# One transformer block on one core: sums of the down projection's weight blocks moved behind the attention, and a planner's priorities set anew

## The chip, the core and the metric

The kernel runs on one core of a Trainium2 chip. The core has five engines with an instruction queue each: TensorE (PE in the profile; PEld is its loading of weights), VectorE (DVE), ScalarE (ACT), GpSimd (POOL) and SyncE (SP). SP does nothing but issue DMAs; ACT and POOL issue some as well. An engine works through its queue in order, so an instruction that waits holds up all that stand behind it. The metric is the device time of one execution in microseconds (us); lower is better.

## The reference

One block of a transformer with 512 tokens and a width of 1024, all in 32-bit floats:

```python
h = x
u = rmsnorm(h, norm_mix_g) @ w_in
c_q, c_kv, k_rope, q_nsa, kv_cmp, kv_slc, kv_win, gate_logits = split(u)
o_mla = mla_mixer(c_q, c_kv, k_rope, ...)        # latent attention, 8 heads
o_nsa = nsa_mixer(q_nsa, kv_cmp, kv_slc, kv_win, gate_logits, ...)   # sparse attention: compressed, selected, window
mixed = concatenate([rmsnorm(o_mla), rmsnorm(o_nsa)])
h = h + mixed @ w_out
f = rmsnorm(h, norm_ffn_g)
h = h + (silu(f @ w_gate) * (f @ w_up)) @ w_down   # w_gate, w_up: 1024 x 2816, w_down: 2816 x 1024
return rmsnorm(h, final_norm_g)
```

## The kernel before

Nearly every product is split for accuracy: each operand is parted into a rounded high part and the rest (w_hi and w_lo, xTh and xTl), and one product becomes three matmuls, which one helper writes at L168, L169 and L170. A weight block is loaded (w_raw, by SP at L405), cast to its high part (w_hi, L392) and subtracted to its low part (w_lo, L394 on DVE or L395 on POOL).

The stages follow each other in the trace as follows. From 0 to about 20 us x is normalized (scaling at L334) and transposed (L349), with products of the norm's gains with ones (L426) and small choice products (L535) in between. To about 105 us come the projections: x times the blocks of w_in, 24 matmuls of 512 columns for a block of 128 columns of weights; qs is the scaled query (L371). Among them is the hidden layer of the compressed keys and values (L715 and L717). Then follow the sparse attention (scores L894 and L895, scaling s on POOL at L840, transposes L845, values L879), and from about 197 us the latent attention's heads (scores L1185). w_out is multiplied first with the sparse half (oTh and oTl), then with the latent half (omh and oml); L1305 adds the result to h, and the norm's mean of the latent half is the product L1272. From about 300 us to 622 the feed-forward part runs: gate and up by a scheme that makes seven block products of eight (its loads at L1532, ACT's casts at L1580, DVE's subtractions at L1396, into w_unit), then down by a like scheme.

For down the scheme needs sums and differences of blocks of w_down. They are made memory to memory by sum_weights: six groups u of four sums T1, T3, T2, T4, each of 512 KB, as a copy from w_down into a tensor T in DRAM, issued by ACT (L1356), and a DMA that adds a second block onto it, issued by POOL (L1357). Each copy waits for the addition ahead of it, and the first for the loading of the gates (ga_loaded), so the 24 pairs are one chain; in the profiled execution it goes from 56.6 to 497 us. The loads of w_down's blocks in the second half (L1705) wait for their sum.

The order of the instructions is made by a planner in the kernel's own code. Each step is a Job with one or more ways (engine, estimated duration, function that writes the instructions), the jobs that it waits for, a priority and the buffers that it takes and frees. Plan.run keeps a clock for each engine; for each it picks, among the jobs whose start is earliest, the one with the lowest priority number, and writes its instructions there and then. So priorities and estimated durations fix every engine's order when the kernel is built, and the chip follows it whatever the real durations are. The dictionary PRI holds about thirty of the priorities and, as pdve, ppool and pact, an amount added for a job that could run on another engine too. SP also loads the bias (bn from ldr, L595) and the gates' rows (ga from gdr, L603) back out of DRAM, in eight DMAs at a time.

Of the kernel before, what the change touches and what calls it, by code (L numbers as in the profile page):

```python
# [13 lines left out]
OP = mybir.AluOpType  # L14
# [40 lines left out]
class Plan:  # L55
# [11 lines left out]
    def add(self, ways, fn=None, after=(), pri=0.0, takes=(), frees=(), lag=None):  # L67

        if fn is not None:
            ways = [(ways[0], ways[1] * (1.07 if ways[0] == "pe" and ways[1] < 1374 else 1.0), fn)]  # L70
        j = Job(ways, [a for a in after if a is not None], pri, takes, frees, lag)
        self.jobs.append(j)
        return j
# [13 lines left out]
    def run(self):  # L87
        busy = {}
        clock, ready, waiting = {"dma": 3500.0, "dma2": 3000.0}, [], list(self.jobs)
        while waiting or ready:  # L90
# [4 lines left out]
            for j in ready:  # L95
                if any(len(self.slots[s]) < j.takes.count(s) for s in j.takes):
                    continue
                for way in j.ways:
                    e = way[0]
                    issue = 1150 if e in ("dma", "dma2") else 0  # L100
                    t = max([clock.get(e, 0.0)] + [a.seen(e) + issue for a in j.after] + [min(self.slots[s]) + issue for s in j.takes])
                    best.setdefault(e, []).append((t + (PRI.get("p" + str(e), 0) if len(j.ways) > 1 else 0), j.pri, j, way, t))
            assert best, "no job can go on"
            picks = []
            for e, c in best.items():
                t0 = min(x[0] for x in c)
                picks.append(min((x for x in c if x[0] <= t0 + PRI["slack"]), key=lambda x: x[1]))
            _, _, j, way, t = min(picks, key=lambda x: (x[0], x[1]))
# [11 lines left out]

PRI = dict(k0=-5.4, q0=-12.1, v=51.3, ck=-13.0, k1=8.0, cv=-9.5, q1=-9.4, q2=-38.5, q3=12.6, mla=38.1, out=180.9, slack=0, pdve=20.1,
           ppool=72.3, pact=310.9, wload=-10.3, wsplit=-28.4, mkeys=-2.4, lat=-20.5, cmp=-18.4, cuse=94.3, use=17.0, sout=77.2, seven=183.9,
           xoff=-26.6, xstep=-35.5, bias=-61.8, sums=912.1, bout=-82.5, loff=-25.8, woff=-217.5, wstep=301.5)


@with_exitstack
def block_kernel(ctx: ExitStack, tc: tile.TileContext, I, out):
    nc = tc.nc  # L130
    ve, se, pe, gp, sy = nc.vector, nc.scalar, nc.tensor, nc.gpsimd, nc.sync
# [140 lines left out]
    add = plan.add  # L272
    late = {}

    def t_act(n, sb=False):
        return (95 if sb else 55) + 0.833 * n
# [4 lines left out]
    def t_dve(n):  # L281
        return 70 + 1.042 * n
# [18 lines left out]
    def load(dst, src, pri, after=()):  # L301
        n = int(np.prod(dst.shape)) * 4
        return add(("dma", max(n / 360.0, 480)), lambda: sy.dma_start(dst, src), after, pri, lag=950)
# [86 lines left out]
    def split_pieces(h, l, raw, n, after, pri, takes=(), frees=()):  # L390

        j = add([("act", t_act(n, True), lambda: se.copy(h(), raw())), ("dve", t_copy(n), lambda: ve.tensor_copy(h(), raw()))],  # L392
                None, after, pri, takes=takes)
        return add([("dve", t_dve(n), lambda: ve.tensor_tensor(l(), raw(), f(h()), op=OP.subtract)),  # L394
                    ("pool", t_pool(n), lambda: gp.tensor_tensor(l(), raw(), f(h()), op=OP.subtract))], None, [j], pri, frees=frees)  # L395

    def weight(pl, srcs, shape, pri, raw, part, nraw, npart, after=(), pieces=2, parts=None):
# [9 lines left out]
        def piece(c):  # L407
            return slice(c * shape[0] // pieces, (c + 1) * shape[0] // pieces)

        def room():  # L410
            w["h"], w["l"] = parts() if parts else [pl().tile([P] + list(shape), F32R, name=nm, tag=nm, bufs=npart) for nm in ("w_hi", "w_lo")]

        j = w["load"] = add(("dma", n * P * 4 / 360.0), start, after, pri + PRI["wload"], takes=[raw], lag=950)
        j = w["room"] = add((None, 0), room, [j], pri + PRI["wsplit"], takes=[part])
        return w, [split_pieces(lambda c=c: w["h"][:, piece(c)], lambda c=c: w["l"][:, piece(c)], lambda c=c: w["raw"][:, piece(c)], n // pieces,
                                [j], pri + PRI["wsplit"] + 0.1 * c, frees=[raw] if c == pieces - 1 else ()) for c in range(pieces)]

# [13 lines left out]
    def load_wl(u):  # L431
        sy.dma_start(wl_raw[:, u, :, 0:416], win[:, 2 * u:2 * u + 2, 0:416])
        sy.dma_start(wl_raw[:, u, :, 416:440], win[:, 2 * u:2 * u + 2, C_GATE:C_END])

    wl_ready = []
    for u in range(4):
        j = add(("dma", 1300), lambda u=u: load_wl(u), pri=-97 + (u if u < 3 else 4), lag=950)
        wl_ready += [split_pieces(lambda u=u, k=k: wl_parts[u][0][:, k], lambda u=u, k=k: wl_parts[u][1][:, k], lambda u=u, k=k: wl_raw[:, u, k],
                                  440, [j], -95 + PRI["woff"] + PRI["wstep"] * u) for k in range(2)]
    x_loaded = [x0] + [[load(xt[t], xv[:, t, :], (-94, -92, -91)[t - 1])] * 2 for t in range(1, NT)]  # L440
# [165 lines left out]
    ga_loaded = add(("dma", 3800), load_ga, bias1 + [p2_open], 6, lag=950)  # L606
# [475 lines left out]
    for t in range(NT):  # L1082
# [3 lines left out]
        def go(d=d, ts=ts):  # L1086
            d["o"] = bank("mm")
            mm3(d["o"], kvTh[:, ts], kvTl[:, ts], flat(late["uvh"]), flat(late["uvl"]), True, True)

        j = add(("pe", 640), go, uv_ready + lat_done, mpri + t, takes=["mm"])  # L1090
        vm_ready += split_values(lambda t=t: late["vm"][:, t], lambda d=d: d["o"].rearrange("p (h d) -> p h d", h=H), S, [j], mpri + t)
    for q in range(2):
        qc = slice(384 * q, 384 * q + 384)
        for t in range(NT):
# [17 lines left out]
            j = add(("pe", 480), lambda go=go: go(0), [uq_ready[q][0]] + lat_done, pri, takes=["mm"])  # L1112
            j = add(("pe", 480), lambda go=go: go(1), [j, uq_ready[q][1]], pri)
            j = add(("act", t_act(256)), lambda qd=qd, ov=ov: se.copy(qd()[:, :, 0:64], ov()[:, :, 0:64]), [j], pri)
            j = add(("dve", 480), rope, [j], pri, frees=["mm"])
# [192 lines left out]
    for nh in range(2):  # L1308
        for t in range(NT):
# [7 lines left out]
            j = None  # L1317
            for k in range(4):
                j = add(("pe", 640), lambda k=k, go=go: go(k), [j, wo[2 * nh + k // 2][1][k % 2]] + sparse_jobs, opri + 4 * nh + t, takes=["mm"] if k == 0 else (),
                        frees=["part2"] if t == NT - 1 and k % 2 else ())  # L1320
# [4 lines left out]
    for nh in range(2):  # L1325
        for t in range(NT):
# [7 lines left out]
            j = None  # L1334
            for k in range(4):
                j = add(("pe", 640), lambda k=k, go=go: go(k), [j, wo[4 + 2 * nh + k // 2][1][k % 2]] + latent_jobs, 300 + 4 * nh + t,
                        takes=["mm"] if k == 0 else (), frees=["part2"] if t == NT - 1 and k % 2 else ())
# [3 lines left out]

    wsum, wsum_done = {}, {}

    def sum_weights():
        wd = I["w_down"].rearrange("(q j p) (n c) -> p q j n c", j=2, p=P, n=2)
        last = [ga_loaded]
        for u in range(6):
            qs = slice(2 * u, min(2 * u + 2, 11))
            n = qs.stop - qs.start
            for name in ("T1", "T3", "T2", "T4"):  # L1350
                wsum[name, u] = dram.tile([P * n, 512], F32, name=f"{name}_{u}")
            b = lambda jj, nn, qs=qs: wd[:, qs, jj, nn, :]
            o = lambda name, u=u: wsum[name, u].rearrange("(q p) c -> p q c", p=P)
            for name, first, second in (("T1", lambda b=b: b(0, 0), lambda b=b: b(0, 1)), ("T3", lambda b=b: b(1, 1), lambda b=b: b(0, 1)),
                                        ("T2", lambda b=b: b(0, 0), lambda o=o: o("T3")), ("T4", lambda b=b: b(1, 0), lambda o=o: o("T2"))):
                j = add(("act", 80), lambda o=o, name=name, first=first: se.dma_start(o(name), first()), last, PRI["sums"], lag=8000)  # L1356
                j = wsum_done[name, u] = add(("pool", 1000), lambda o=o, name=name, second=second: gp.dma_start(o(name), second(), accum_op=OP.add, max_dma_last_dim=2048), [j], PRI["sums"], lag=8500)  # L1357
                last = [j]

    sum_weights()  # L1360


    def feed_forward():
# [78 lines left out]
        x_scaled = [ff_norm(t, 303.5 + 4 * t) for t in range(NT)]  # L1442
# [27 lines left out]
        for q in range(2):  # L1470
            pri = 311.5 + 4 * q
            x11, x12, x21, x22 = [lambda t=t, e=e: xn[t][e] for t in (q, q + 2) for e in range(2)]
            d, j = turned(S3, q, [x21, x11], [x_scaled[q][0], x_scaled[q + 2][0]] + mm_free, pri, tag="mm", last=False)
            d, j = turned(S2, q, [x22], [j, x_scaled[q + 2][1]], pri + 0.2, d, "mm", False)
            turned(S4, q, [x12], [j, x_scaled[q][1]], pri + 0.4, d, "mm")
            d, j = turned(A22, q, [x22], [x_scaled[q + 2][1]], pri + 0.1, last=False)
            turned(S1, q, [x21], [j, x_scaled[q + 2][0]], pri + 0.1, d)
        add((None, 0), lambda: None, xs_read, 320, frees=["pt"] + ["s"] * 4)


        def open_late():
            om_ctx.close()
            pl = pool("late", side="right")
            y = pl.tile([P, 2, HS], F32, name="a_end")
            a_src[5, 2], a_src[5, 3] = y[:, 0:1], y[:, 1:2]
            for c in (2, 3):
                raws[1][c] = pl.tile([P, 4, 2 * P], F32, name=f"b_late{c}")
# [113 lines left out]
        for q, v in order_of:  # L1601
# [11 lines left out]
            o, first = INTO[v]  # L1613
# [29 lines left out]
            elif v == "P2":  # L1643
                j = add(("dve", t_dve(512)), lambda d=d, tmp=tmp: ve.tensor_tensor(tmp("c1")(), tmp("c1")(), d["Y"], op=OP.add), [T[q, "c1"], p_last], hp, frees=["pv"])
# [3 lines left out]
            elif v == "P3":  # L1648
                j = add(("dve", t_dve(512)), lambda d=d, tmp=tmp: ve.tensor_tensor(tmp("u2")(), tmp("u2")(), d["Z"], op=OP.add), [T[q, "u2"], p_last], hp, frees=["mm"])
# [119 lines left out]
        for u in range(NU):  # L1769
            pri = 600 + 10 * u  # L1770
            rest[u] = down_lefts(u, pri)
            for v in PH[0]:
                w, j = down_weight(u, v, pri)
# [35 lines left out]
        for u, v in units:  # L1809
# [3 lines left out]
            w, j = down_weight(u, v, pri)  # L1813
# [127 lines left out]
```

## Time and profile before

| what | value |
|---|---|
| median of 3 runs | 644.17 us (644.1 to 644.45) |
| profiled execution | 642.98 us, span 641.1 us |
| granted PE clock, mean | 0.992 |
| PE busy | 609.1 us, 95% of the span |
| DVE, ACT, POOL busy | 520.9, 369.6, 177.0 us |
| DMA moved | 92.75 MB |

All durations below come from the one profiled execution. Its span is the time from its first to its last instruction; 1.9 us lie around it. A row of a timeline gives the start, the duration, the engine and line, the operation with output and inputs, and in brackets how long the engine was idle before it and for what. A group of rows gives a count, busy time and mean in ns. Matmuls overlap, so a row's duration is longer than the distance to the next.

### The profile page before, as it was taken

To read this page: it belongs to the slowest core of one execution; us is meant where nothing else is said; L and a number is where in the kernel's file an instruction comes from. 1 tells how busy PE (TensorE), PEld (TensorE's weight loads), DVE (VectorE), ACT (ScalarE), POOL (GpSimd) and SP (SyncE) were. 2 spreads that over 40 slices of the span, in tenths; PEclk is the share of its full clock that TensorE was granted. 3 is DMA by queue.
4 is the path that set the end of the run, shared out by engine and by line. 5 is a ranking of instruction groups with operands and counts; after the bars stand their busy time and mean duration, and the time that the engine had idled before them with its cause. 6 is when DMAs were issued, how large, how long until landed. Compare 5 with 4: busy or idle time off the path is not lost.

```text
span 641.1 us, 11228 instructions
## 1 busy us (share of the span) xinstructions
PE 609.1 (95%) x3973; PEld 540.8 (84%) x3973; DVE 520.9 (81%) x1078; ACT 369.6 (58%) x767; POOL 177.0 (28%) x252
## 2 busy tenths in 40 slices
PE   4999889999999989999999999999999999999994
PEld 2878677988887767887999999999999998888883
DVE  5856788589999898659978777887778999978846
ACT  3532248589898876334754455454455586458434
POOL 3632356357965683325000000000000000000003
PEclk9999899999999999999999999999999999999997
DMA  9635762463331863475584666655544366456503
GB/s 280 124 88 149 171 159 64 87 161 71 63 71 34 265 166 63 132 228 166 148 215 128 185 181 186 168 121 151 163 151 130 88 196 198 146 181 194 183 1 131
DMA packets 76297, 92.75 MB, mean 145 GB/s; under 512 B 10240, under 2 KB 49584, under 8 KB 76242
## 3 DMA queue, kind: packets, MB, share of 16 engines
q1 hardware_dynamic: 63248, 67.53, 34.2%
q0 software_dynamic: 6080, 11.75, 11.5%
q10 hardware_dynamic: 6914, 12.75, 6.9%
q8 instruction: 31, 0.51, 0.3%
q14 instruction: 24, 0.20, 0.1%
HBM read 89.24 MB, written 25.85 MB: 180 GB/s over the span
## 4 chain that ended last, share of the span: by engine, by line
PE 71%; DVE 13%; issue 5%; ACT 4%; DMA 3%; POOL 2%; SPq 0%; POOLq 0%; ACTq 0%; DVEq 0%
PE mm L168 9%; PE mm L170 9%; PE mm L169 9%; PE sc L170 7%; PE sc L169 7%; PE sc L168 7%; PE pv L169 3%; PE pv L170 3%; PE pv L168 3%; PE tp L845 3%; DMA w_raw<-in_w_in_dram 2%; PE pv L879 2%; DVE s L829 2%; DVE ptl L853 2%; PE tp L168 1%
## 5 line engine op out<-in xcount | busy, mean ns | idle before, releaser
L170 PE MATMUL sc<-fh,w_unit 128*128 128x256 f32 x352 | 98.5, 280 | 0.0
L168 PE MATMUL sc<-fh,w_unit 128*128 128x256 f32 x352 | 98.5, 280 | 0.0
L169 PE MATMUL sc<-fl,w_unit 128*128 128x256 f32 x352 | 98.2, 279 | 0.0
L1396 DVE TENSOR_TENSOR w_unit<-b_raw,w_unit 128x1024 fp32r<-128x1024 f32 (+1 forms) x54 | 63.9, 1183 | 25.5 <-ACT w_unit L1580 15.2
L169 PEld LDWEIGHTS sc<-fl,w_unit 128*128 128x128 f32 x352 | 66.2, 188 | 0.0
L170 PEld LDWEIGHTS sc<-fh,w_unit 128*128 128x128 f32 x352 | 66.1, 188 | 0.0
L168 PEld LDWEIGHTS sc<-fh,w_unit 128*128 128x128 f32 x352 | 65.8, 187 | 0.0
L834 ACT ACTIVATE s<-s,m 128x128 f32<-128x128 f32 (+3 forms) x96 | 53.6, 559 | 11.7 <-DVE m L829 11.2
L1396 DVE TENSOR_TENSOR w_unit<-b_first,w_unit 128x1024 fp32r<-128x1024 f32 (+1 forms) x34 | 40.0, 1175 | 24.4 <-ACT w_unit L1580 18.1
L840 POOL TENSOR_SCALAR s<-s,l,gates 128x128 f32<-128x128 f32 (+3 forms) x64 | 41.7, 667 | 30.2 <-DVE l L837 21.3
L170 PE MATMUL mm<-fh,w_unit 128*128 128x256 f32 x176 | 49.3, 280 | 0.0
L168 PE MATMUL mm<-fh,w_unit 128*128 128x256 f32 x176 | 49.1, 279 | 0.0
L169 PE MATMUL mm<-fl,w_unit 128*128 128x256 f32 x176 | 49.1, 279 | 0.0
L853 DVE TENSOR_TENSOR ptl<-tp,pth 128x128 fp32r<-128x128 f32 (+3 forms) x96 | 44.3, 482 | 3.6 <-ACT pth L850 2.9
L395 POOL TENSOR_TENSOR w_lo<-w_raw,w_hi 128x512 fp32r<-128x512 f32 x27 | 36.1, 1344 | 39.6 <-DVE w_hi L392 17.6
L850 ACT ACTIVATE pth<-tp 128x128 fp32r<-128x128 f32 (+3 forms) x96 | 39.0, 431 | 7.9 <-PE tp L845 4.7
L845 PE MATMUL tp<-ident,s 128*128 128x128 f32 x240 | 40.5, 277 | 2.2 <-DVE ptl L853 1.6
L1357 POOL DMA_DIRECT2D T<-T x12 | 13.1, 1095 | 99.1 <-DMA T<-in_w_down_dram 98.7
L1580 ACT CAST w_unit<-b_raw 128x1024 fp32r<-128x1024 f32 x32 | 33.6, 1051 | 11.4 <-PE pv L169 5.9
L1856 POOL TENSOR_SCALAR ss<-ss 128x1 f32<-128x1 f32 x9 | 3.2, 357 | 133.6 <-ACT xo L1853 133.5
L1357 POOL DMA_DIRECT2D T<-in_w_down_dram x12 | 13.4, 1117 | 85.9 <-DMA T<-in_w_down_dram 85.9
L845 PEld LDWEIGHTS tp<-ident,s 128*128 128x128 f32 x240 | 27.4, 140 | 9.7 <-POOL s L840 3.5
(366 smaller groups left out, 1976.6 us busy)
## 6 DMA issues: line engine op xcount, KB each, us to landing
T<-in_w_down_dram ACTq DMA_DIRECT2D x20, 512.0 KB, 4.1
b_first<-in_w_gate_dram SPq DMA_DIRECT2D x12, 512.0 KB, 4.4
b_raw<-in_w_up_dram SPq DMA_DIRECT2D x12, 512.0 KB, 6.5
T<-in_w_down_dram POOLq DMA_DIRECT2D x10, 512.0 KB, 6.8
T<-T POOLq DMA_DIRECT2D x10, 512.0 KB, 5.9
b_raw<-in_w_gate_dram SPq DMA_DIRECT2D x10, 512.0 KB, 4.2
b_late<-in_w_up_dram SPq DMA_DIRECT2D x10, 512.0 KB, 4.8
b_raw<-in_w_down_dram SPq DMA_DIRECT2D x10, 512.0 KB, 3.5
```

The costliest lines, as they stand in the source:

```text
L168: pe.matmul(o, lh, rh, start=start, stop=False, **kw)
L169: pe.matmul(o, lh, rl, start=False, stop=False, **kw)
L170: pe.matmul(o, ll, rh, start=False, stop=stop, **kw)
L395: ("pool", t_pool(n), lambda: gp.tensor_tensor(l(), raw(), f(h()), op=OP.subtract))], None, [j], pri, frees=frees)
L834: se.activation(c["s"][:, 0:n], c["s"][:, 0:n], AF.Exp, bias=c["m"], scale=-1.0, accum_out=c["l"])
L840: eng.tensor_scalar(c["s"][:, 0:n], c["s"][:, 0:n], c["l"], gate(), op0=OP.mult, op1=OP.mult)
L845: pe.transpose(c["tp"][:, j * P:(j + 1) * P], c["s"][:, j * P:(j + 1) * P], ident)
L850: se.activation(c["dh"], c["src"], AF.Copy)
L853: ve.tensor_tensor(c["dl"], c["src"], f(c["dh"]), op=OP.subtract)
L1357: j = wsum_done[name, u] = add(("pool", 1000), lambda o=o, name=name, second=second: gp.dma_start(o(name), second(), accum_op=OP.add, max_ ...
L1396: return add(("dve", t_dve(n)), lambda: ve.tensor_tensor(dst(), a(), b(), op=op), after, pri, **kw)
L1580: j = add(("act", t_act(n, True)), lambda: se.copy(w["p"][0], b()), [rw] + need, pri + 5)
```

## The change

sum_weights is called inside feed_forward, after the norm's scaled parts are written, with the last of them as its start. A copy no longer waits for the addition ahead of it, but for the start and the copy two places before. An addition waits for its own copy and the addition ahead of it. All of PRI's numbers but slack are new.

```diff
-PRI = dict(k0=-5.4, q0=-12.1, v=51.3, ck=-13.0, k1=8.0, cv=-9.5, q1=-9.4, q2=-38.5, q3=12.6, mla=38.1, out=180.9, slack=0, pdve=20.1,
...
+PRI = dict(k0=-18.71, q0=-49.36, v=205.05, ck=-15.95, k1=-16.99, cv=-11.94, q1=-29.34, q2=-51.07, q3=18.07, mla=41.51, out=708.57, slack=0, pdve=5.6,
...
-    def sum_weights():
+    def sum_weights(start):
...
-        last = [ga_loaded]
+        copied_in = []
+        last, wait = [], [start]
...
-                j = add(("act", 80), lambda ...: se.dma_start(o(name), first()), last, PRI["sums"], lag=8000)
-                j = wsum_done[name, u] = add(("pool", 1000), lambda ...: gp.dma_start(o(name), second(), accum_op=OP.add, max_dma_last_dim=2048), [j], PRI["sums"], lag=8500)
+                j = add(("act", 80), lambda ...: se.dma_start(o(name), first()), wait + copied_in[-2:-1], PRI["sums"], lag=9000)
+                copied_in.append(j)
+                j = wsum_done[name, u] = add(("pool", 1000), lambda ...: gp.dma_start(o(name), second(), accum_op=OP.add, max_dma_last_dim=2048), [j] + last, PRI["sums"], lag=8500)
                 last = [j]
-
-    sum_weights()
...
+        sum_weights(x_scaled[3][1])
```

What this does to the engines' orders is seen at three places. First SP's queue in the projections; w_raw from in_w_in is a block of w_in, from in_nsa_cmp_w_k a block of the compression weights. Before:

```order
L405 DMA w_raw<-in_w_in_dram 128x8x128
L405 DMA w_raw<-in_nsa_cmp_w_k_dram 128x8x128 x2
L595 DMA bn<-ldr 32x2x512 x8
L405 DMA w_raw<-in_w_in_dram 128x8x128
L603 DMA ga<-gdr 16x8x56 x8
L405 DMA w_raw<-in_w_in_dram 128x8x128
L405 DMA w_raw<-in_nsa_cmp_w_v_dram 128x8x128 x2
```

and after:

```order
L405 DMA w_raw<-in_w_in_dram 128x8x128 x3
L595 DMA bn<-ldr 32x2x512 x8
L405 DMA w_raw<-in_w_in_dram 128x8x128
L603 DMA ga<-gdr 16x8x56 x8
L405 DMA w_raw<-in_nsa_cmp_w_k_dram 128x8x128 x2
L405 DMA w_raw<-in_w_in_dram 128x8x128
L405 DMA w_raw<-in_nsa_cmp_w_v_dram 128x8x128 x2
```

Two blocks of w_in have moved ahead of the bias and the gates, the compression weights behind them. PE's order changes with it: before, the hidden layer (L715, L717, from the windows rr) follows after three projections,

```order
L168 MATMUL mm<-xTh,w_hi 128x512
L169 MATMUL mm<-xTl,w_hi 128x512
L170 MATMUL mm<-xTh,w_lo 128x512
L715 MATMUL mm<-rr,w_hi 128x136
L717 MATMUL mm<-rr,w_lo 128x68
```

and after, six projections stand in a row, and the first scores of the sparse attention follow at once (the hidden layer comes nine matmuls behind them):

```order
L168 MATMUL mm<-xTh,w_hi 128x512
L169 MATMUL mm<-xTl,w_hi 128x512
L170 MATMUL mm<-xTh,w_lo 128x512
L894 MATMUL sc<-kh,qs 128x128
L895 MATMUL sc<-kl,qs 128x128
```

Before, the hidden layer separates the projections; after, the scores do. The second place is the end of the attention on PE. Before, the mean's product (L1272) is followed by six products of three matmuls with oT before the first with om (omh, oml); after, one is left:

```order
L170 MATMUL mm<-w_hi,oTl 128x512
L1272 MATMUL mm<-ones_68,sqm 128x2 x4
L168 MATMUL mm<-w_hi,oTh 128x512
L169 MATMUL mm<-w_lo,oTh 128x512
L170 MATMUL mm<-w_hi,oTl 128x512
L168 MATMUL mm<-w_hi,omh 128x512
L169 MATMUL mm<-w_lo,omh 128x512
L170 MATMUL mm<-w_hi,oml 128x512
```

The other five have moved to places between the latent heads. Ahead of L1272, 21 matmuls with oT stand behind the last values product in both orders. The third place is POOL. Before, the additions onto T stand among the attention's work, such as the scaling of s:

```order
L840 TENSOR_SCALAR s<-s,l,gates 128x128 x2
L1357 DMA T_0_132<-T_0_131 128x2x512
L840 TENSOR_SCALAR s<-s,l,gates 128x256 x2
L840 TENSOR_SCALAR s<-s,l,gates 128x512
L840 TENSOR_SCALAR s<-s,l,gates 128x384 x2
```

and after, all 24 stand in a row behind the norm's roots (L1429 and the lines around it):

```order
L1429 TENSOR_TENSOR xr<-ss,mhalf 128x1
L1431 TENSOR_SCALAR xr<-xr 128x1
L1359 DMA T_0_130<-in_w_down_dram 128x2x512
L1359 DMA T_0_131<-in_w_down_dram 128x2x512
L1359 DMA T_0_132<-T_0_131 128x2x512
```

None is left ahead of the feed-forward part. On ACT the copies stand there too, in couples between its casts. At the start, PE's second product of the gains (L426) now follows four choice products (L535), before it followed none and two choice products came behind both. The rest of the orders differs in many small places; from the first product with om to the end PE's order is the same.

More of the change, by code (lines that the diff above doesn't have):

```diff
@@ L119, in run @@
         self.jobs = []
-PRI = dict(k0=-5.4, q0=-12.1, v=51.3, ck=-13.0, k1=8.0, cv=-9.5, q1=-9.4, q2=-38.5, q3=12.6, mla=38.1, out=180.9, slack=0, pdve=20.1,
-           ppool=72.3, pact=310.9, wload=-10.3, wsplit=-28.4, mkeys=-2.4, lat=-20.5, cmp=-18.4, cuse=94.3, use=17.0, sout=77.2, seven=183.9,
-           xoff=-26.6, xstep=-35.5, bias=-61.8, sums=912.1, bout=-82.5, loff=-25.8, woff=-217.5, wstep=301.5)
+PRI = dict(k0=-18.71, q0=-49.36, v=205.05, ck=-15.95, k1=-16.99, cv=-11.94, q1=-29.34, q2=-51.07, q3=18.07, mla=41.51, out=708.57, slack=0, pdve=5.6,
+           ppool=29.34, pact=192.57, wload=-38.41, wsplit=-86.02, mkeys=245.43, lat=-172.29, cmp=-19.94, cuse=34.19, use=13.36, sout=232.76,
+           seven=164.94, xoff=-151.88, xstep=-63.88, bias=-169.42, sums=905.55, bout=-207.35, loff=-71.72, woff=-438.76, wstep=585.98)
 @with_exitstack
@@ L1355, in sum_weights @@
                                         ("T2", lambda b=b: b(0, 0), lambda o=o: o("T3")), ("T4", lambda b=b: b(1, 0), lambda o=o: o("T2"))):
-                j = add(("act", 80), lambda o=o, name=name, first=first: se.dma_start(o(name), first()), last, PRI["sums"], lag=8000)
-                j = wsum_done[name, u] = add(("pool", 1000), lambda o=o, name=name, second=second: gp.dma_start(o(name), second(), accum_op=OP.add, max_dma_last_dim=2048), [j], PRI["sums"], lag=8500)
+                j = add(("act", 80), lambda o=o, name=name, first=first: se.dma_start(o(name), first()), wait + copied_in[-2:-1], PRI["sums"], lag=9000)
+                copied_in.append(j)
+                j = wsum_done[name, u] = add(("pool", 1000), lambda o=o, name=name, second=second: gp.dma_start(o(name), second(), accum_op=OP.add, max_dma_last_dim=2048), [j] + last, PRI["sums"], lag=8500)
                 last = [j]
-    sum_weights()
     def feed_forward():
```

## The prediction

> **What bounds the kernel now.** I read the engine totals first, then the stages, then what waits in the stages that are not full.
>
> ```profile
> PE 609.1 (95%) x3973; PEld 540.8 (84%) x3973; DVE 520.9 (81%) x1078; ACT 369.6 (58%) x767; POOL 177.0 (28%) x252
> ```
>
> ```profile
> 0.00:20.00 20.00, 11.74 (x30) 7.64 (x31) 12.07 (x33) 7.80 (x19) 9.81 (x19) 1.00 0.92 271
> ...
> 60.00:100.00 40.00, 34.66 (x192) 29.43 (x191) 31.62 (x78) 15.44 (x38) 17.20 (x22) 0.96 0.63 149
> ...
> 140.00:264.00 124.00, 118.48 (x755) 98.29 (x754) 116.32 (x405) 103.67 (x298) 85.41 (x125) 1.00 0.42 110
> 264.00:300.00 36.00, 35.00 (x167) 28.50 (x167) 24.49 (x33) 14.11 (x28) 11.90 (x15) 1.00 0.65 181
> 300.00:622.00 322.00, 321.09 (x2316) 301.64 (x2316) 267.16 (x326) 175.21 (x230) 14.30 (x15) 1.00 0.55 158
> ```
>
> After a window and its length come the busy us of PE, PEld (PE's weight loads), DVE, ACT and POOL, the granted PE clock, the DMA engines' busy share and GB/s. From 300 to 622 us PE is busy 321.1 of 322: half of the span, with nothing to win there and only something to lose. In the attention (140 to 264) DVE is at 94% and ACT at 84%. PE's holes lie at the start (8.3 us), at 60 to 100 (5.3 us) and in the attention (5.5 us). The hole at 60 to 100 has a cause that the change touches. First what SP waited for, then the chain of work there (start, length, what):
>
> ```profile
> SPq L603 <- DMA T<-in_w_down_dram: 5.0, 1, 5.0
> ```
>
> ```profile
> 51.97 0.23 PE mm L169
> ...
> 56.05 0.23 PE mm L169
> ...
> 56.55 4.27 DMA T<-in_w_down_dram
> ...
> 60.84 0.30 SPq L603
> ...
> 62.67 3.77 DMA w_raw<-in_w_in_dram
> ...
> 66.56 0.43 DVE w_hi L392
> ...
> 67.02 0.70 DVE qs L371
> ```
>
> The first copy of a sum (T, issued by ACT at 56.55) holds up SP's eight gate loads (L603) by 5.0 us, though the two share no data. The weight load queued behind them starts only at 62.67; DVE stands at its cast (w_hi), with the scaling qs behind it, and PE needs qs. PE's rows, and the window after its gap:
>
> ```profile
> 67.86 0.77 PE L168 MATMUL mm<-xTh,w_hi 128*128 128x512 f32 x1 [2.42 <-DVE qs L371]
> ...
> 71.47 0.39 PE L168 MATMUL mm<-xTh,w_hi 128*128 128x512 f32 x1
> ```
>
> ```profile
> 67.90:71.30 3.40, 3.40 (x9) 2.68 (x10) 3.19 (x11) 0.70 (x2) 0.87 (x2) 0.54 0.21 62
> ```
>
> PE is idle for 2.42 us and then runs at a clock of 0.54: from 67.86 to 71.47 it starts nine matmuls of 512 columns, 0.401 us apart. Undisturbed they follow each other every 0.227 us (51.97 to 56.05 in the chain: 18 steps in 4.08).
>
> **The change, part by part.** The sum is made on the profiled execution, 642.98 us (span 641.1). The median shown is 644.17, 1.19 above it; that is added at the end.
>
> (a) No sum is issued ahead of the feed-forward part, so SP's wait for T goes, and with it PE's gap and the slow nine: 2.4 + (3.61 − 9 × 0.227 = 1.6) = **−4.0**. SP also issues two more w_in blocks ahead of the bias loads, so the block that was late (the fifth) no longer stands behind the gate loads at all.
>
> The Trainium skill (TensorE: Matmul & The Clock Gate, Part 1: The HAM clock gate) puts the danger at idle gaps of PE above some 3.4 us, seen through a free-running window. By that rule (a) would be −2.4 and the time 1.6 higher; the trace has the slow clock after a gap of 2.42, so it decides against the rule as a threshold.
>
> (b) PE now takes six projections in one row, and only then the hidden layer of the compressed keys; the first sparse scores come some 10 us of PE work earlier. What comes early can wait for DVE. Such waits now:
>
> ```profile
> 86.06 0.72 PE L925 MATMUL sc<-kc,qs 128*128 128x64 f32 x5 [1.01 <-DVE qs L371]
> ...
> 93.99 0.44 PE L957 MATMUL tp<-ident,s 128*128 128x128 f32 x2 [0.54 <-DVE s L970]
> 96.56 0.47 PE L168 MATMUL mm<-xTh,w_hi 128*128 128x512 f32 x1 [1.12 <-DVE vc L369]
> ```
>
> They make 2.7 us. If the reordering removes all three: −2.7; if it makes one more stall like that of (a): +4.0. I take **+1.0**, one wait more of the size of these rows, to which a score that comes early is nearest.
>
> (c) At the start the second product of the gains (L426) now stands behind four choice products (before, two came after both), and ACT issues the loads of bias and gates earlier. PE there:
>
> ```profile
> 8.44 0.70 PE L535 MATMUL tp<-choice,txp 33*8 33x320 f32 x2
> 11.22 1.11 PE L349 MATMUL tp<-ident,x 128*128 128x128 f32 x4 [2.08 <-DVE x L334]
> ```
>
> Four choice products of 0.35 us, 1.4 in all, now stand ahead of the second half of the gains, which x's second scaling (L334) needs, and PE waits for that; two of them, 0.7, were on PE's way to the transposes (L349) anyway. Bounds: −0.7 (all of it falls into the 2.08, and two choice products fewer stand later, where PE is full) and +2.1 (a whole wait of the size of this row again). I take **+1.0**, between 0.7 and 1.4.
>
> (d) At the passage to the output projection, PE's group of products of w_out with oT behind the last values product, DVE's last work on om, and PE's first product with it:
>
> ```profile
> L168 PE MATMUL mm<-w_hi,oTh 128*128 128x512 f32 x13 | 5.2, 401 | 0.0
> ```
>
> ```profile
> 267.42 0.75 DVE L1235 SCALAR_TENSOR_TENSOR oml<-ofm,og,omh 128x512 fp32r<-128x512 f32 x1
> 268.30 0.75 DVE L1305 SCALAR_TENSOR_TENSOR h<-mm,r,h 128x512 f32<-128x512 f32 x1
> ```
>
> ```profile
> 274.50 0.40 PE L168 MATMUL mm<-w_hi,omh 128*128 128x512 f32 x1
> ```
>
> With L169 and L170 that makes 39 matmuls; the changed order leaves 24, so 15 × 0.227 = 3.4 us of PE's work move into the latent heads, where DVE sets the pace and PE has its 5.5 us of holes. The products with om can follow: oml is ready at 268.2 and PE comes to it at 274.5, so 6.3 us of room take the 3.4. Against it stands DVE's addition to h (L1305), one for twelve matmuls: 15/12 × 0.75 = 0.9 more in the stage where DVE is the bound. Bounds: −3.4, and +0.9 if PE's holes there can't be filled. I take **−2.5**.
>
> (e) The issues of the sums leave the attention:
>
> ```profile
> L1356 ACTq DMA_DIRECT2D T<-in_w_down_dram x24: 497/559/687, 56.6 to 491.5; - x24
> ```
>
> ```profile
> L1357 POOL DMA_DIRECT2D T<-in_w_down_dram x12: 828/1147/1287, 72.3 to 461.6; - x12
> L1357 POOL DMA_DIRECT2D T<-T x12: 814/1135/1202, 112.3 to 496.6; - x12
> ```
>
> ```profile
> L845 PEld LDWEIGHTS tp<-ident,s 128*128 128x128 f32 x240 | 27.4, 140 | 9.7 <-POOL s L840 3.5
> ```
>
> ```profile
> 278.31 0.63 ACT L1420 ACTIVATE xns<-h 128x512 f32<-128x512 f32 x1 [2.99 <-DMA T<-in_w_down_dram]
> ```
>
> 24 accumulations from 72 to 497 are one in some 18 us, so about half of the pairs lie ahead of 300 us: 12 × 0.56 on ACT and 12 × 1.14 on POOL, 20 us on two engines that are not the bound. What PE's weight load waits for POOL's scaling of s is 3.5 in all, the upper end of the gain; 0 is the lower, if DVE sets the pace alone. I take **−1.0**, since few of the scalings have an accumulation ahead of them. ACT's wait of 2.99 at 278 shows on no PE row (35.0 of 36 busy in that stage): nothing.
>
> (f) In the feed-forward part all 24 pairs lie between some 305 and 500 us, and ACT issues two copies at a time between its casts. How far weight loads run ahead, what the DMA engines do there, and what the two queues of the sums take in all:
>
> ```profile
> 351.26 0.37 SPq L1532 DMA_DIRECT2D b_first<-in_w_gate_dram  x1
> ```
>
> ```profile
> 378.97 1.23 DVE L1396 TENSOR_TENSOR w_unit<-b_first,w_unit 128x1024 fp32r<-128x1024 f32 x1 [1.60 <-ACT w_unit L1580]
> ```
>
> ```profile
> 300.00:360.00 60.00, 59.09 (x502) 58.64 (x502) 49.49 (x59) 33.42 (x46) 6.46 (x7) 1.00 0.67 178
> 360.00:420.00 60.00, 60.00 (x512) 60.00 (x511) 48.45 (x56) 30.07 (x37) 3.40 (x3) 1.00 0.62 171
> ```
>
> ```profile
> q0 software_dynamic: 6080, 11.75, 11.5%
> q10 hardware_dynamic: 6914, 12.75, 6.9%
> ```
>
> A block loaded at 351.26 is read by the DVE row at 378.97, and by ACT's cast (some 1.6 us) ahead of it, at about 377: 26 us, of which some 6 are the landing and 20 are slack. Of the span of 641 the copies (q10) take 44 us of all DMA engines, 1.8 each, the accumulations (q0) 74, 3.1 each; q10 holds some of ACT's other loads, so this is too much rather than too little. From 305 to 420 there were about six pairs, 29 us; now there are all 24 copies and 11 to 14 of the chained accumulations, 78 to 87 us. That is 49 to 58 more in 115, on a share of 0.65: 1.07 to 1.15, a backlog of 8 to 17 us by 420, still inside the 20. I take **0**. The chain of accumulations, 24 × 8 us behind 305, ends at about 500; the second half reads the sums in order from 491 on, the last block some 60 us later.
>
> Sum: −4.0 + 1.0 + 1.0 − 2.5 − 1.0 + 0 = −5.5: 637.5 on the profiled execution, **638.7** beside the median.
>
> **The rivals.**
>
> B, a larger gain: the three waits of (b) go (−2.7 instead of +1.0) and (c) is nothing: −5.5 − 3.7 − 1.0 = −10.2, 634.0. For it: all three come of DVE's order, which is new. Against it: DVE has the same work, earlier.
>
> C, no change that can be measured (within 0.2%, 1.3 us, about what a measurement of this kernel can tell): the weight block is late for another reason, such as buffers that PE still reads, so (a) is nothing, and half of (d) is lost: −5.5 + 4.0 + 1.25 = −0.25, 643.9. For it: DVE's cast and SP's loads also wait for buffers there, unseen by PE. Against it: the chain goes through T's landing without a break.
>
> D, slower: in the new order of the front PE stands still for over 2 us at new places, each with the slow clock behind it, 4.0 apiece as in (a). In place of the 1.0 of (b), one gives −2.5, two +1.5 (645.7), three +5.5 (649.7); it decides from two on. For it: six projections in a row need a weight block, split by DVE and POOL, every 24 × 0.227 = 5.5 us. Against it: the chain from 51.97 to 56.05 has this pace without a gap.
>
> E, slower in the feed-forward part: with no accumulation held back and the sums ahead of the loads, the backlog is 30 instead of 17, 10 beyond the slack: 638.7 + 10 = 649. ACT standing at a copy whose turn hasn't come would do the same through its casts. For it: PE has no reserve there. Against it: half of the sums do no harm there today.
>
> The Trainium skill (DMA: Bandwidth & Descriptors, Queues, rings and completion order) says that each DMA engine serves its queues in turn, a packet at a time, so that weight loads have no precedence over the sums; this is E's mechanism, and no row here tells how far it delays a load.
>
> **How the numbers follow.** The forecast (a gain of 1.3 to 8) has 0.48, B 0.18, C 0.12, D 0.15, E 0.07: faster 0.66, same 0.12, slower 0.22. The time is the forecast's, 638.7; its own range is 636 to 642.5. With B below 633.5 (some 0.08), and D from three stalls on and E (0.12) left out, the range is 633.5 to 646.
>
> **What would show it.** In the changed profile SP's wait for T is gone, and between 45 and 100 us PE has no gap of 2 us and no window at half clock (a). Waits for DVE ahead of the first scores make some 4 us (b). PE's first product with x is within 1 us of its old time plus 1 (c). The first product with omh starts at about 269 instead of 274.5 (a to e together), with 24 matmuls between it and the last values product (d). From there on the length is the same and PE stays full (f). A new gap above 2 us ahead of it, or PE below 99% in the feed-forward part, would prove the forecast wrong.

## The result, and the profile after

The change makes the kernel slower: 650.92 us median of four runs (650.34 to 652.81) against 644.17, a ratio of 1.0109 with a 95% interval of 1.0088 to 1.0130. The forecast was 638.7 with a range to 646.0. The profiled execution of the changed kernel takes 652.81 us with a span of 651.0, 9.9 more than the 641.1 of before. These two executions lie further apart than the medians, 6.75 us: the changed kernel's is the slowest of its four, and the old kernel's is faster than the three others of it. In the changed kernel the lines of the sums, and those behind line 1479, are by one or two higher than before; the others are the same.

The stages first, with the columns of the prediction's windows (after the window and its length: PE, PEld, DVE, ACT, POOL, PE clock, DMA share, GB/s). The feed-forward window ends eight microseconds later, since everything is late:

```profile
0.00:20.00 20.00, 10.96 (x26) 5.07 (x27) 11.83 (x31) 7.29 (x17) 8.78 (x17) 1.00 0.88 259
20.00:60.00 40.00, 35.36 (x158) 29.36 (x158) 22.33 (x67) 14.36 (x48) 11.32 (x15) 0.96 0.38 74
60.00:100.00 40.00, 38.08 (x178) 31.60 (x177) 30.08 (x60) 13.39 (x30) 12.94 (x12) 0.94 0.44 118
100.00:140.00 40.00, 38.62 (x261) 34.60 (x259) 28.35 (x101) 23.41 (x70) 19.23 (x31) 0.93 0.15 41
...
300.00:630.00 330.00, 328.19 (x2354) 307.40 (x2353) 275.19 (x338) 181.10 (x241) 34.96 (x37) 1.00 0.69 194
```

The feed-forward part is as full as it was: PE is busy 99.5% of this window, and 321.08 of the 322 us from 310 to 632, where it was 321.09 of 322. The loss lies ahead of it, and most of it in the first 60 us. PE's first product with a block of w_in and its first with omh, after the change:

```profile
53.65 0.39 PE L168 MATMUL mm<-xTh,w_hi 128*128 128x512 f32 x1
```

```profile
284.29 0.40 PE L168 MATMUL mm<-w_hi,omh 128*128 128x512 f32 x1
```

and the first of these before:

```profile
44.08 0.50 PE L168 MATMUL mm<-xTh,w_hi 128*128 128x512 f32 x1
```

So PE is 9.6 us late at 53.65, and still 9.8 late at 284.29 (it was 274.50). From there to the end of the span are 366.7 us, before 366.6. Nothing is lost behind, and nothing that the prediction hoped to win between the two has come out on balance.

What makes the start late shows on ACT's timeline (ACTq is an issue of a DMA), after the change:

```profile
19.96 0.84 ACTq L543 DMA_DIRECT2D ldr<-brow  x1
20.27 0.61 ACT L322 ACTIVATE xTh<-x 128x512 fp32r<-128x512 f32 x1
...
20.90 0.71 ACTq L543 DMA_DIRECT2D ldr<-brow  x1
21.70 4.62 ACTq L545 DMA_DIRECT2D gdr<-brow  x1
26.37 0.58 ACT L539 ACTIVATE brow<-tp 8x504 f32<-8x504 f32 x1 [5.39 <-issue]
26.98 3.73 ACTq L545 DMA_DIRECT2D gdr<-brow  x1
30.83 0.63 ACT L322 ACTIVATE xTh<-x 128x512 fp32r<-128x512 f32 x1 [3.88 <-issue]
...
31.46 1.06 ACT L363 ACTIVATE xTh<-tp 128x512 fp32r<-128x512 f32 x2
```

and before:

```profile
24.09 0.71 ACTq L543 DMA_DIRECT2D ldr<-brow  x1
...
44.98 0.30 ACTq L545 DMA_DIRECT2D gdr<-brow  x1
...
46.24 0.27 ACTq L545 DMA_DIRECT2D gdr<-brow  x1
```

The same two issues of the gates' rows (gdr) take 0.30 and 0.27 us before, and 4.62 and 3.73 after. What changed is what stands ahead of them: now the two writes of the bias (ldr) are just issued, before, the later of them was issued at 24.09, 21 us ahead. Behind the gates' writes on ACT stand the square sum of x's fourth tile (L322; the third tile's, at 20.27, stands ahead of them) and two casts of x's transposed tiles (L363). The rows that wait for these, on POOL and DVE, and PE's next transposes, which wait for DVE's scaling behind that row:

```profile
31.72 0.26 POOL L329 TENSOR_SCALAR ss<-ss 128x1 f32<-128x1 f32 x1 [9.18 <-ACT xTh L322]
```

```profile
32.07 0.69 DVE L369 TENSOR_TENSOR xTl<-tp,xTh 128x512 fp32r<-128x512 f32 x1 [10.94 <-ACT xTh L363]
```

```profile
33.52 0.83 PE L349 MATMUL tp<-ident,x 128*128 128x128 f32 x4 [2.51 <-issue]
```

A window of PE's table (PE busy, clock, DMA share, GB/s) tells how fast the DMA engines worked off the bias writes in that time:

```profile
25.00:30.00 5.00, 3.43 (x12) 1.00 0.46 49
30.00:35.00 5.00, 2.49 (x11) 0.88 0.45 48
```

48 to 49 GB/s, less than a fifth of the 259 in the first 20 us: at that rate two writes of 320 KB take some 13.5 us. PE's clock falls there as well, to 0.88 in the second window and 0.78 in the one behind it, which makes 1.7 us.

The other loss is at the hidden layer of the compressed keys, the place of (b):

```profile
92.27 0.30 PE L715 MATMUL mm<-rr,w_hi 128*128 128x136 f32 x1 [1.64 <-DVE rr L369]
```

```profile
95.00:100.00 5.00, 5.00 (x19) 0.52 0.40 107
100.00:105.00 5.00, 4.49 (x23) 0.79 0.38 105
105.00:110.00 5.00, 5.00 (x24) 0.66 0.21 48
```

A gap of 1.64 us, and behind it a clock that is missing 0.48, 0.21 and 0.34 of five microseconds each, 5.1 us. The last 1.7 of these stand behind a second gap, of 0.51 us ahead of the scores at 104.51 (L925).

### The profile page after: what moved, and what is told of

The parts are those of the page before. It is cut to its first block, busy times and chain, and to the rows that moved or that the text cites. A ratio compares the mean times of both kernels' runs of the same rounds, so it can differ in the third digit from the quotient of the medians.

```text
span 651.0 us, 11222 instructions
## 1 busy us (share of the span) xinstructions
PE 616.6 (95%) x3973; PEld 546.5 (84%) x3973; DVE 522.3 (80%) x1077; ACT 368.3 (57%) x767; POOL 177.4 (27%) x253
## 4 chain that ended last, share of the span: by engine, by line
PE 73%; DVE 15%; ACT 4%; issue 3%; ACTq 1%; DMA 1%; POOL 1%; SPq 0%; POOLq 0%; DVEq 0%
PE mm L168 10%; PE mm L170 10%; PE mm L169 10%; PE sc L170 7%; PE sc L169 7%; PE sc L168 7%; PE pv L170 3%; PE pv L169 3%; PE pv L168 3%; DVE s L829 3%; PE tp L845 2%; PE pv L879 2%; DVE ptl L853 2%; PE tp L168 1%; PE tp L169 1%
## 5 line engine op out<-in xcount | busy, mean ns | idle before, releaser
L845 PE MATMUL tp<-ident,s 128*128 128x128 f32 x240 | 42.1, 280 | 2.4 <-DVE l L837 0.9
L1716 ACT CAST w_unit<-b_raw 128x1024 fp32r<-128x1024 f32 (+1 forms) x22 | 21.4, 975 | 23.8 <-PE mm L170 8.2
```

The source lines that it names most:

```text
L845: pe.transpose(c["tp"][:, j * P:(j + 1) * P], c["s"][:, j * P:(j + 1) * P], ident)
L1716: j = add(("act", t_act(512 * n, True)), lambda: se.copy(w["p"][0], raw()), [rw, ld], pri + 1)
```

## The experiments

All ratios are to the kernel before, run beside each on the same chip; the times of before scatter there by 0.6 to 1.2%, so the intervals decide, and places are read from the traces.

**e1: the gates' writes alone moved back.** The changed kernel, with the two issues waiting for the third latent product:

```diff
-        return add(("act", 80), out, [j] + wl_ready, PRI["bout"], ...)
+        return add(("act", 80), out, [j] + wl_ready + (wl_used[2:3] if c1 > 640 else []), PRI["bout"], ...)
```

> The changed kernel with one thing moved: ACT issues the two writes of the gates' rows (gdr) after the third of the four latent products of x, not directly behind the two writes of the bias (ldr). Theory 1 (ACT's queue stands 4.62 and 3.73 us at these two issues, and the whole front with it): the first product with a w_in block comes 7 to 10 us earlier than at 53.65, and the time is 641 to 644. Rival (the new order of the start is slow by itself: choice products and casts placed early): not more than 3 us come back, 648 or above.

Measured: 643.92 us, 0.9990 [0.9976, 1.0005]. The two issues on ACT, and PE's first product with w_in:

```profile
43.72 0.31 ACTq L545 DMA_DIRECT2D gdr<-brow  x1
44.08 0.29 ACTq L545 DMA_DIRECT2D gdr<-brow  x1
```

```profile
48.62 0.39 PE L168 MATMUL mm<-xTh,w_hi 128*128 128x512 f32 x1
```

The issues are short again, and 1.0109 − 0.9990 = 1.2%, 7.7 us, come back. The first product came 5.0 us earlier, less than the 7 to 10 expected, so something else in the start holds it too (e6, e11).

**e2: the opposite, on the kernel before.** Choice products, scaling and writes of the gates' rows written directly behind the second bias write:

```diff
+        if c1 > 640:
+            early.append([product, negated, out])
+            product = negated = out = lambda: None
+        elif c0 == 320:
+            first = out
+            def out():
+                first()
+                for step in range(3):
+                    for fns in early:
+                        fns[step]()
```

> The kernel before with the opposite: the choice products, the scaling and the two writes of the gates' rows written directly behind the second write of the bias, nothing else changed. Theory 1: ACT's two issues take about 4 us each there instead of 0.3, ACT is held for some 8 us at 24 us, and the time rises by 5 to 10 us, to 649 to 654. Rival (order of the start): the issues stay at 0.3 us, and the time rises by at most 1.5 us for the two products taken early, to 646.

Measured: 650.77 us, 1.0105 [1.0083, 1.0127]. ACT's row and PE's first product with w_in:

```profile
24.68 4.78 ACTq L547 DMA_DIRECT2D gdr<-brow  x2
```

```profile
49.51 0.40 PE L168 MATMUL mm<-xTh,w_hi 128*128 128x512 f32 x1
```

Moving these two writes, with their products and scalings, costs 1.05% in the old kernel, about what moving them back won in the changed one. They take 4.8 us together, not 4 each. A likely reason is that the first of the two bias writes had been issued 8.1 us ahead of them, in the changed kernel 1.7. The loss isn't all ACT's: behind this wait PE's clock is 0.50 from 30 to 40 us, where it was 1.00 before.

**e3 and e4: the two halves of the change apart.** e3 is the kernel before with the sums moved, e4 the changed kernel with the sums in their old chain. In each, jobs without instructions keep the planner's old times, so that PE's and SP's orders are those of the kernel that it comes from:

```diff
+    def place_holders():
+        last = [ga_loaded]
+        for u in range(24):
+            j = add(("act", 80), lambda: None, last, PRI["sums"], lag=8000)
+            j = add(("pool", 1000), lambda: None, [j], PRI["sums"], lag=8500)
+            last = [j]
...
+        sum_weights(x_scaled[3][1])
```

> The kernel before with the sums alone moved into the feed-forward part; its own priorities, and places without work in the planner where the sums were, so that all other orders stay. The prediction's steps (a) and (e): SP's wait of 5.0 us for T, PE's gap of 2.42 and the slow clock behind it go, 4 to 5 us faster, 639 to 640. Rival 1: the gap has another cause or another takes its place, 643 to 645. Rival 2: the sums hurt the feed-forward part, above 646.

> The changed kernel with the new priorities, but the sums back in one chain through the attention, from the gates' loading on. Theory 1: the late front is all of the loss and comes of the priorities, so this kernel is as slow as the changed one or slower by what the sums cost in the attention: 651 to 654. Rival (the sums in the feed-forward part are the loss): 643 to 646.

Measured: e3 640.47 us, 0.9939 [0.9917, 0.9961]; e4 655.95 us, 1.0175 [1.0154, 1.0196]. The moved sums win 0.61% under the old priorities and 1.0175 − 1.0109 = 0.66% under the new ones, some 4 us both times; the new priorities lose 11. e4 is slower than the 651 to 654 expected. In e3's trace SP's gate loads no longer wait for T, and PE's gap and the windows around and behind it read

```profile
67.19 0.47 PE L168 MATMUL mm<-xTh,w_hi 128*128 128x512 f32 x1 [1.34 <-DVE qs L371]
```

```profile
65.00:70.00 5.00, 3.66 (x20) 1.00 0.48 144
70.00:75.00 5.00, 5.00 (x24) 1.00 0.60 169
```

A gap of 1.34 stays where there were 2.42, and in this execution no slow clock follows. In e4 the old wait is back:

```profile
SPq L603 <- DMA T<-in_w_down_dram: 4.9, 1, 4.9
```

**e5: e3 with out=708.57**, meant for step (d).

> The kernel of e3 (before, the sums in the feed-forward part) with one more number of the change, out=708.57 in place of 180.9: the products of w_out with oT move as in the changed kernel, 24 instead of 39 behind the last values product. The prediction's step (d): 2.5 us faster than e3, a ratio of 0.990 to before. Rival: the holes that they fill belong to DVE's pace and the time is e3's, 0.994, or the additions on DVE cost more, 0.996.

Measured: 643.78 us, 0.9958 [0.9924, 0.9993], whose interval leaves out the 0.990 and holds both rivals. It says little about step (d) all the same, as the order shows: here the 15 matmuls with oT went behind the first products with om, not between the latent heads, so the run doesn't test what it was meant for. The first product with omh comes early, at 267.52, and 371.9 us still follow it instead of 366.

**e6: the changed kernel with the old start**, eight priorities put back:

```diff
-xoff=-151.88, xstep=-63.88, bias=-169.42, bout=-207.35, loff=-71.72, woff=-438.76, wstep=585.98, lat=-172.29
+xoff=-26.6, xstep=-35.5, bias=-61.8, bout=-82.5, loff=-25.8, woff=-217.5, wstep=301.5, lat=-20.5
```

> The changed kernel with the eight priorities of the start (xoff, xstep, bias, bout, loff, woff, wstep, lat) as before: choice products, casts and both DMA writes of the start in their old places, everything later as changed. Theory 1 extended: the start of the changed kernel cost some 12 us, 8 by the gates' writes and 4 by the order of the rest; the first product with w_in is back at 44 to 45 us, and the time is 639 to 641, level with e3, since the stall at the hidden layer (1.6 us and half a clock for some 10 us behind it) eats what (d) gains. Rival: the later part of the changed order is slow too, 643 or above.

Measured: 642.72 us, 0.9972 [0.9953, 0.9991]; PE's first product with w_in and with omh:

```profile
44.44 0.50 PE L166 MATMUL mm<-xTh,w_hi 128*128 128x512 f32 x1
```

```profile
273.32 0.40 PE L166 MATMUL mm<-w_hi,omh 128*128 128x512 f32 x1
```

(line numbers are two lower here, and in e8 and e11). The start is where it was, and with it the kernel is faster than before. The time lies between the 639 to 641 expected and the rival's 643, and it isn't below e3's: the new middle part wins nothing on balance.

**e7: the gates' writes issued by POOL** instead of ACT, at the same early place.

```diff
-                se.dma_start(gdr[:, c0 - 640:c1 - 640], d["row"])
+                gp.dma_start(gdr[:, c0 - 640:c1 - 640], d["row"])
```

> The changed kernel with the two writes of the gates' rows issued by POOL at the same early time, ACT left with the two bias writes. Theory 1a (ACT's own queue is backed up by the bias writes, which the DMA engines work off at 48 GB/s): POOL's issue takes the 1.1 us of its other DMAs, ACT is not held, and the time is that of e1, 0.997 to 1.001 of before. Rival 1b (the DMA engines themselves are full, so any queue is held): POOL stands for 4 us or the time stays at 1.007 or above.

Measured: 646.00 us, 1.0014 [0.9990, 1.0038]; POOL's two rows:

```profile
21.24 0.63 POOL L545 DMA_DIRECT2D gdr<-brow  x1 [2.04 <-ACT brow L539]
23.56 0.51 POOL L545 DMA_DIRECT2D gdr<-brow  x1 [1.70 <-ACT brow L539]
```

With the bias writes in flight as before, POOL's issues take 0.63 and 0.51 us. So an issue from POOL is not held in that time, one from ACT is; the time is next to the 0.997 to 1.001 of theory 1a and below rival 1b's 1.007.

**e8: e3 with the new priorities of the attention only.**

> The kernel of e3 with the changed kernel's priorities of the attention and of the choice between engines (mla, out, mkeys, cmp, cuse, use, sout, seven, pdve, ppool, pact), but the old ones for the start and the projections. It tells (d) and the attention's order from the projections' order. Expected: as e5, 0.988 to 0.992 of before. Rival: the attention's new order costs what e5 gains, 0.994 to 0.998.

Measured: 646.67 us, 1.0030 [1.0015, 1.0045], on the rival's side but above the range of both. As in e5, products with oT stand behind the first with om (270.07, and 372.6 us after it), so this too tells little of the heads. Its front is e3's, matmul for matmul, and has the same gap ahead of the same product, but the clock differs:

```profile
66.84 0.76 PE L166 MATMUL mm<-xTh,w_hi 128*128 128x512 f32 x1 [1.34 <-DVE qs L369]
```

```profile
65.00:70.00 5.00, 3.66 (x13) 0.66 0.57 167
```

So whether a gap of this length brings the slow clock is not settled by its length. The start shows it again: the kernels with the old start have a gap of 1.77 to 1.80 us at about 30 us, and behind it the clock from 30 to 35 us is 0.66 in e3, e5 and e9, and 1.00 in e6, e8 and e11.

**e9: e6 with PE's gap filled** by seven matmuls that nobody reads:

```diff
                 c_["hid"] = bank("mm")
+                if kv == 0:
+                    spare = bank("pv")
+                    for _ in range(7):
+                        pe.matmul(spare, xTh[:, 0, 0:P], xTh[:, 0, :], start=True, stop=True)
```

> The kernel of e6 with one addition: ahead of the hidden layer's first matmul, where PE stands 1.63 us, seven matmuls of 512 columns into an unused bank, whose result nobody reads (1.6 us). Theory 2 (the gap is what brings the slow clock behind it, and the slow clock costs more than the gap): no window below a clock of 0.95 from 60 to 110 us, and 3 to 5 us less than e6, 0.990 to 0.993 of before. Rival (the clock drops for another reason, or the short matmuls behind are the cause): the time of e6, 0.997, or more by the 1.6 us.

Measured: 640.75 us, 0.9953 [0.9937, 0.9969], against e6's 0.9972: the difference, 1.2 us, is less than the 3 to 5 expected, and the intervals overlap, so the time alone proves no gain. The clock shows one; the windows of e6, then those of e9:

```profile
85.00:90.00 5.00, 5.00 (x29) 0.72 0.09 20
90.00:95.00 5.00, 4.48 (x25) 0.94 0.69 192
```

```profile
85.00:90.00 5.00, 5.00 (x32) 1.00 0.30 73
90.00:95.00 5.00, 4.03 (x26) 1.00 0.50 138
```

In e9 the clock is 1.00 throughout from 60 to 115 us. Of the seven traces with a gap of 1.61 to 1.64 us at this place, six (e1, e4, e6, e7, e11 and the changed kernel) have the slow clock within 3.3 us behind it, and in e10 it stays at 1.00 up to 100 us. The mean clock of e9's nine runs is 0.990 to 0.995, of e6's twelve 0.981 to 0.992. So at this place the gap is what brings the clock down, though not every time. That costs 5 × (0.28 + 0.06) = 1.7 us in e6's profiled execution; the changed kernel's lost 3.4 behind this gap.

**e10: the bias writes issued by SP**, the gates' writes left on ACT.

```diff
-                se.dma_start(ldr[:, :, c0:c1], ...)
+                sy.dma_start(ldr[:, :, c0:c1], ...)
```

> The changed kernel with the two bias writes (ldr) issued by SP at their early place, ahead of the first loads of w_in, and the two gates' writes left on ACT right behind them. Theory 1a (a queue holds its own engine while what it issued before is not worked off): ACT issues the gates' writes in 0.3 us each; now SP, which issues loads behind the bias writes, is held instead, its next issues take some 4 us, and the time lies between e1 and the changed kernel, 0.999 to 1.008. Rival (writes of the gates' rows are slow whenever the bias writes are in flight, from any queue): ACT's issues take 4 us again, 1.009 or more.

Measured: 648.78 us, 1.0075 [1.0058, 1.0092]. SP's queue and ACT's two issues:

```profile
16.56 1.67 SPq L543 DMA_DIRECT2D ldr<-brow  x2
18.28 9.07 SPq L405 DMA_DIRECT2D w_raw<-in_w_in_dram  x2
27.45 5.22 SPq L691 DMA_DIRECT2D posr<-in_nsa_cmp_pos_v_dram  x1
```

```profile
20.34 0.29 ACTq L545 DMA_DIRECT2D gdr<-brow  x1
21.69 2.38 ACTq L545 DMA_DIRECT2D gdr<-brow  x1
```

The hold moves with the writes: now SP stands, 9.07 us for two loads and 5.22 for one of 8 KB, where it took 1.01 and 0.93 in the changed kernel. ACT's first issue is short, but its second takes 2.38, which theory 1a does not explain; what SP's and ACT's issues share stays open.

**e11: e1 with the old priority of the choice products**, bias=-61.8.

> The kernel of e1 with the old priority of the choice products (bias=-61.8), so that they and the bias writes stand where they stood before; the other six priorities of the start stay as changed. It parts the 5 us between e1 (first product with w_in at 48.6) and e6 (44.4). If the choice products are what delays the start, the first product with w_in is at 44 to 45 and the time that of e6, 0.997; if it is the order of the casts and of x's tiles, it stays at 48 and the time at 0.999 to 1.002.

Measured: 643.18 us, 0.9982 [0.9969, 0.9995], the first product with w_in at 43.98 us. In this trace the changed casts cost nothing at the start. In time the difference to e1, 0.08%, is inside the intervals, though at that product it is 4.6 us. e1's profiled execution was the slowest of its runs (646.76), so the 4.6 are rather too much.

A part of them is PE's own pace. A product of 440 columns ahead of the first with w_in, in e1 and in e11:

```profile
27.48 0.57 PE L168 MATMUL mm<-wl,xTh 128*128 128x440 f32 x1
```

```profile
17.09 0.36 PE L168 MATMUL mm<-pth,xTl 128*128 128x440 f32 x1
```

Such matmuls start 0.37 us apart at first and 0.20 apart later, though the clock column gives 1.00 for both. The pace changes at 28.3 us in e1 and at 16.6 in e11, so 14 more of them are slow in e1: 14 × 0.17 = 2.4 us. The early choice products alone don't bring this about, for e10 has them too and changes at 19.3. So what holds the start besides the gates' writes stays open.

## Why the prediction was wrong

The chain of kernels adds up in ratios, each step with one part of the change more: the sums moved 0.9939 (e3); the new middle 0.9972 (e6); the new start without the early gates' writes 0.9990 (e1); all of it 1.0109.

(a) The sums: **right** in the mechanism, down to the clock. Removing the wait for T won 0.61%, 3.9 us, where (a) and (e) made 5.0. In the trace of e3 (a) is −2.7, 1.1 of the gap and 1.6 of slow clock: 1.34 us of the gap stayed, because DVE is late with qs there anyway, and the prediction had put the whole gap down to T. (e) is hardly visible: between the last wait of (b) and the first product with omh e3 is another 0.4 us faster. Rival C fails on it.

(b) The middle: the kind was right, the size too small. The three old waits are gone and a new one came, of 1.64 us, in front of the hidden layer: DVE does early scores and casts ahead of rr. The prediction chose "one wait more of the size of these rows" and so left out the slow clock, which it had kept for its upper bound of +4.0. With the clock the term is 1.6 + 5.1 − 2.7 = +4.0 in the changed kernel (1.7 of the 5.1 behind the second, smaller gap), and 1.6 + 1.7 − 2.7 = +0.6 in e6, whose order is the same there: from below the +1.0 up to the bound, as the clock falls.

(c) The start is **the step that failed**: +1.0 with bounds of −0.7 and +2.1, and it measured 53.65 − 44.08 = +9.6. By the ratios it is 1.0109 − 0.9972 = 1.37%, 8.8 us, of which the gates' writes make 7.7 (e1). The prediction did name that ACT issues "the loads of bias and gates" earlier (they are the writes that those loads read back), and gave it no term of its own. It left out that an issue can become longer when it is moved, here from 0.3 to 4.62 and 3.73 us, and it asked what stands behind a DMA on ACT's queue for E, not here. The trace of before has the gates' writes 21 us behind the bias writes and so never shows them together: a cost that it doesn't show, for which a bound was needed. The bound that was taken came from a row of another kind, PE's wait for DVE; for the thing that was moved, ACT's place behind the bias writes, there was none. PE's slow pace of the start, too, lasted longer: to 30.4 us and again from 33.8 to 37.2, where it ended at 19.8 before, so 31 instead of 14 of the matmuls of 440 columns are slow. That is some 2.9 us, an estimate at 0.17 each; how much of it lies inside PE's waits for ACT is not shown.

(d) From the first score of a latent head to the first product with omh, after and before (first and last start in the group's row):

```profile
L1185 PE MATMUL sc<-mk,q x64: 272/483/595, 208.7 to 269.1; 96*128 96x128 f32 x16, 96*128 96x256 f32 x16, 96*128 96x384 f32 x16, 96*128 96x512 f32 x16
```

```profile
L1185 PE MATMUL sc<-mk,q x64: 272/483/595, 197.6 to 251.4; 96*128 96x128 f32 x16, 96*128 96x256 f32 x16, 96*128 96x384 f32 x16, 96*128 96x512 f32 x16
```

75.6 us after, 76.9 before: 1.3 won where 2.5 were forecast, and other work moved across the first score too, so this hints at (d) more than it measures it. No run isolates it.

(f) Zero was **right**, and E with its 0.07 did not come. The sums do crowd the DMA engines, as the issue rows of the page show (median us to landing, last), after and before:

```profile
T<-in_w_down_dram ACTq DMA_DIRECT2D x20, 512.0 KB, 9.0
b_first<-in_w_gate_dram SPq DMA_DIRECT2D x12, 512.0 KB, 6.8
```

```profile
T<-in_w_down_dram ACTq DMA_DIRECT2D x20, 512.0 KB, 4.1
b_first<-in_w_gate_dram SPq DMA_DIRECT2D x12, 512.0 KB, 4.4
```

Copies land after 9.0 us instead of 4.1 and gate blocks after 6.8 instead of 4.4. The 20 us of slack take it. The terms as the traces give them, +9.6 for (c), −2.7 for (a), +4.0 for (b) and −1.3 for (d), add up to 9.6 of the 9.9 us between the two profiled executions.

D was the rival that came nearest: the front became the bound. But its mechanism, several PE gaps of over 2 us, comes near at one place only, (b), with a gap of 1.64; the greater part is an engine held at an issue, which no case had. That its 649.7 for three gaps lies close to the measured 650.92 is luck.

The Trainium skill (DMA: Bandwidth & Descriptors, Issuing engines are not separate DMA queues) says that issuing on several engines saves only the time to initiate a DMA, usually small beside the transfer. Here that time was 8.4 us of ACT for two writes of 15.8 KB, and POOL instead of ACT brought back 0.95% (e7).

e3 is the best version found, 0.9939: the sums moved, the priorities left. e9 is level with it (0.9953).

## What to carry to other kernels

An issue of a DMA is an instruction whose length can depend on what was issued shortly before, here by the same engine above all (e10 shows a case across two engines): where a change brings issues of one queue together, ask how long the earlier ones take to be worked off, and which compute instruction stands behind them. A change of two things is best taken apart with jobs that keep their place but write nothing; here it showed a win of 4 us under a loss of 11. And a PE gap has the price of the gap plus the slow clock behind it, if one follows, which in these traces was anything from nothing to three times the gap.

## What the runs showed of the hardware that was not expected

- ACT's issue of a small DMA took 4.62 and 3.73 us behind two writes of 320 KB moving at 48 GB/s, and 0.27 to 0.31 with those done (before, e1, e6). Issued by POOL in the same time it took 0.51 to 0.63 (e7). With the large writes on SP's queue, ACT's second issue still took 2.38 (e10).
- The slow clock came after six of seven gaps of 1.61 to 1.64 us at the hidden layer (not in e10) and cost 1.7 us (e6), some 3.4 (e1, e7, e11, the changed kernel) or 5.1 (e4) behind them; after a gap of 1.34 it came in e8 and not in e3, with the same instructions on PE up to there, and after gaps of 1.77 to 1.80 in three kernels of six.
- At the start PE ran at about half its later pace (matmuls of 440 columns 0.37 us apart instead of 0.20) while the clock column gave 1.00. This ended at 19.8 us before, at 30.4 in the changed kernel and at 16.3 to 28.3 in the others.
